# The first norm of a hybrid layer: all low parts on VectorE, the first two results' steps in between

## The chip, the cores and the metric

The kernel runs on one core of one Trainium2 chip. The core has five engines that each work through their own queue in program order and wait for each other by semaphores: TensorE (PE in the profile; PEld are its weight loads), VectorE (DVE), ScalarE (ACT), GpSimd (POOL) and SyncE (SP, which here only issues transfers). The metric is the device time of one execution in microseconds.

## The reference

One layer on 512 tokens of width 1024, batch 1, float32:

```
h = rmsnorm(x, norm1)
proj = h @ w_in            # q, k, v of A; beta, alpha; gates; f, i, q of B; g_a, g_b
o_a = gated_delta_rule(...)     # 8 heads of 128, chunkwise with a triangular solve
o_b = hgrn2_recurrence(...)     # 8 heads of 128, state with per-channel decay
x = x + (sigmoid(g_a) * (o_a @ w_a) + sigmoid(g_b) * (o_b @ w_b)) @ w_out
h2 = rmsnorm(x, norm2)
x = x + peer(h2)           # product-key top-16 experts of 16384, 8 heads
return rmsnorm(x, final_norm)
```

rmsnorm is x * rsqrt(mean(x * x) + 1e-6) * g. Only its first use, ahead of `w_in`, matters here, and the two recurrences that read the projections.

## The kernel before, in words

Rows are kept transposed: `xT` is eight chunks (c = 0 to 7) of 128 channels by 512 tokens. A float32 product is made of three matmuls on rounded parts: `hhi` and `whi` are the rounded values, `hlo` and `wlo` what the rounding left, and `piece` (line 505) issues whi by hhi, wlo by hhi and whi by hlo for one chunk. The eight pieces of one unit (128 output columns) sum in one PSUM tile. `w_raw` loads the weights of a unit, `w_cut` (line 501) splits them: ScalarE rounds (`whi`), then VectorE or GpSimd subtracts (`wlo`). Units 0 and 1 were split on VectorE, those behind them on GpSimd.

The first five units (NF = 5: a_k, a_q and three merge-gate units) start before the norm's factor is known. `unscaled` splits x times norm1, the pieces run on that, and the results are multiplied by the factor `rs` afterwards (`rescaled`, line 980). Meanwhile `squares` sums x squared into `acc` (ScalarE squares, VectorE adds), `token_scales` turns the sum into four columns `r4`, and `spread_scales` spreads them over all partitions with diagonals `rd` and matmuls; ScalarE copies the broadcast to `rs`. Then each chunk is scaled properly (`scaled`, VectorE) and split anew (`resplit`, line 456: ScalarE rounds into `hhi`, then the low part, odd chunks on GpSimd, even ones on VectorE). Unit 5 and all behind it read these. The loop at line 1050 issues this: its step k issues one piece, and at set values of k also the steps named above. The steps of the first two results (a_k and a_q: the rescaling, three convolution steps, a tanh and a product, `consume`, line 935) were issued at once at k = 12, ahead of the first `scaled`.

What follows is the mixer. Its order is decided while the program is built: `Flow` (line 136) keeps a clock for each engine from fixed costs, and the loop at line 1108 always issues the next step of that chain whose inputs its clock has ready first. The chains are `setup` (small gates, from the weights wabh and wabl), `branch_a1` and `branch_a2` (branch A; a1 prepares a head, with the transposes of a_k, kn, a_q and a_v in the tile mA; a2 doubles the inverse in iv and then carries the state SA through four blocks), `branch_b` (branch B; seven `level` steps of VectorE and ScalarE with a group of small matmuls in pl each, then the state SB) and `projections` (units 5 to 77, piece by piece). The pieces are what covers the waits of the branches; when they are used up, the branches run bare. A projection is also held back while the head's earlier results are still in use (`allowed`). Behind the mixer come the branch matrices, the second norm, the product-key search and the experts, all in fixed order.

The start times that this order sets on the chip are not Flow's: an engine waits wherever an input is not there.

Of the kernel before, what the change touches and what calls it, by code (L numbers as in the profile page):

```python
# [10 lines left out]
F32 = mybir.dt.float32  # L11
# [7 lines left out]
OP = mybir.AluOpType  # L19
# [6 lines left out]
DC = D // P  # L26
# [45 lines left out]
HEND = 3  # L72
HSTEP = 4
NDMA = 4
LISTS = (10, 26)
HSTART = 18
GPS = 4
# [201 lines left out]
def build(ctx, tc, I, O):  # L279
# [6 lines left out]
    def act(o, i, f, **kw):  # L286
        nc.scalar.activation(o, i, f, **kw)  # L287

    vec, gps, pe = nc.vector, nc.gpsimd, nc.tensor
# [15 lines left out]
    n1, n2, nf = vecs[:, 0:8], vecs[:, 8:16], vecs[:, 16:24]  # L305
# [113 lines left out]
    hhi = hpool.tile([P, DC, T], F32R, name="hhi")  # L419
    hlo = hpool.tile([P, DC, T], F32R, name="hlo")  # L420
# [19 lines left out]
    def token_scales(sums):  # L440
        for tt in range(NC_):
            mm(sums[:, 2 * tt:2 * tt + 2], acc[:, tt * P:(tt + 1) * P], ones2)
        vec.tensor_scalar(r4, sums[:, 0:8:2], 1.0 / D, EPS, OP.mult, OP.add)
        gps.tensor_tensor(r4, r4, mhalf[:, 0:NC_], OP.pow)

    def spread_scales(r, pool):
        rd = pool.tile([P, NC_, P], F32, tag="tmpP", name="rd", bufs=3)
        for tt in range(NC_):
            vec.tensor_scalar(rd[:, tt, :], ident, r4[:, tt:tt + 1], None, OP.mult)
            mm(r[:, tt * P:(tt + 1) * P], onesm, rd[:, tt, :])  # L450

    def scaled(src, g, c, r, t):
        vec.scalar_tensor_tensor(t, src[:, c, :], g[:, c:c + 1], r, OP.mult, OP.mult)
        return t

    def resplit(c, t):
        act(hhi[:, c, :], t, AF.Copy)
        (gps if c % 2 else vec).tensor_tensor(hlo[:, c, :], t, hhi[:, c, :].bitcast(F32), OP.subtract)  # L458

    hm = (hhi, hlo)  # L460
    ps = st2.enter_context(tc.tile_pool(name="ps", bufs=1, space=PSUM))
# [9 lines left out]
    N0 = len(order)  # L471
# [5 lines left out]
    raws, wts = {}, {}  # L477
# [6 lines left out]
    def w_split(raw, eng=gps):  # L484
        hi = wpool.tile([P, DC, UW], F32R, tag="whi", name="whi")
        lo = wpool.tile([P, DC, UW], F32R, tag="wlo", name="wlo")
        act(hi, raw, AF.Copy)
        if eng is None:

            act(lo, hi.bitcast(F32), AF.Copy, scale=-1.0)  # L490
            gps.dma_start(out=lo, in_=raw, accum_op=OP.add)
        else:
            eng.tensor_tensor(lo, raw, hi.bitcast(F32), OP.subtract)  # L493
        return hi, lo

    def w_raw(n):
        if n < len(order):
            kind, j = order[n]
            raws[n] = w_load(I["eut"][j] if kind == "u" else I["wu"][UNITS[kind, j]])

    def w_cut(n):
        if n < len(order):
            wts[n] = w_split(raws.pop(n), vec if n < 2 else gps if n < N0 + NDMA else None)

    def piece(p, w, c, m):
        whi, wlo = w
        mm(p, whi[:, c, :], m[0][:, c, :], c == 0, False)
        mm(p, wlo[:, c, :], m[0][:, c, :], False, False)
        mm(p, whi[:, c, :], m[1][:, c, :], False, c == DC - 1)
# [5 lines left out]
    with ExitStack() as ph:  # L515
        sb = ph.enter_context(tc.tile_pool(name="sb", bufs=1))

        def sbt(tag, bufs=1, shape=(P, T), dt=F32):
            return sb.tile(list(shape), dt, tag=tag, name=tag, bufs=bufs)

        xT = ogA
# [458 lines left out]
        def rescaled(kind, h, p):  # L980
            t = sbt("tmpA", 2)
            vec.tensor_tensor(t, p, rs, OP.mult)
            yield from consume(kind, h, t)
# [5 lines left out]
        def allowed(kind, h):  # L989
            return kind not in HEAD or free[kind] >= h + 1 - RB[kind]  # L990

        def projections():
            def some():
                while late:
                    if next(late[0], True) is None:
                        return
                    late.pop(0)

            for n, (kind, h) in list(enumerate(order[:NPROJ]))[NF:]:
                while not allowed(kind, h):  # L1000
# [6 lines left out]
                for c in range(DC):  # L1007
                    piece(p, wts[n], c, hm)
                    some()
                    if n < NF + NTWO:  # L1010
                        some()
# [6 lines left out]
                        some()  # L1018


        NF = 5
        for t in pbuf:
            gps.memset(t, 0.0)
        gps.memset(keep, 1.0)
# [5 lines left out]
        def squares(c):  # L1030
            sumsq(xT, c, sb, "tmpP", 3, vec if c in ACCV else gps)
# [3 lines left out]
        for c in range(DC):  # L1035
# [6 lines left out]
            if c == W1:  # L1042
                w_cut(1)
        w_cut(2)
        w_raw(3)
        sums = pst("mA", 1)
        r = pst("mC", 1)
        rs = sbt("tmpB", 3)
        t = None
        for k in range((NF - 1) * DC):  # L1050
            n, c = 1 + k // DC, k % DC
            if n > NF - 3:

                c, n = divmod(k - (NF - 3) * DC, 2)
                n += NF - 2
            piece(first[n], wts[n], c, hm)
            if k < DC:
                squares(k)
            if k == 1:
                w_cut(3)  # L1060
                w_raw(4)
            if k >= LB:
                next(lbs, None)
            if k == SC1:
                token_scales(sums)
                w_cut(4)
                w_raw(5)
            if k == SC2:
                spread_scales(r, sb)
                act(rs, r, AF.Copy)  # L1070

                late = [rescaled(*order[n], first[n]) for n in range(NF)]
                pair = late.pop(0), late.pop(0)
                late.insert(0, late.pop())
                next(pair[0])
                next(pair[0])
                for _ in range(8):
                    for g in pair:
                        next(g, None)
            if n == NF - 1:  # L1080
                t2 = scaled(xT, n1, c, rs, sbt("tmpP", 3))
                if c:
                    resplit(c - 1, t)
                t = t2
            if n == NF - 1 and c == 0:
                w_cut(5)
                w_raw(6)
        resplit(DC - 1, t)
        w_cut(6)
        w_raw(7)  # L1090
        for n in range(NF):
# [141 lines left out]
    def cut(o, n, i=0):  # L1233
        return stage[:, o + i * n:o + (i + 1) * n]
# [13 lines left out]
    with ExitStack() as ph:  # L1248
        rt = ph.enter_context(tc.tile_pool(name="rt", bufs=1))

        def rtile(tag, shape, dt=F32, bufs=1):
            return rt.tile([P] + list(shape), dt, tag=tag, name=tag, bufs=bufs)
# [64 lines left out]
        with ExitStack() as p2:  # L1317
# [31 lines left out]
            for u in range(3):  # L1349
                for c in range(DC):  # L1350
# [9 lines left out]
                    if u == 1 and c == 1:  # L1360
                        spread_scales(r, sb)
                        rs = rtile("rs", (T,))
# [6 lines left out]
            t = None  # L1369
            for c in range(DC):  # L1370
                t2 = scaled(x2T, n2, c, rs, cut(6144, T, c % 4))
                if c:
                    resplit(c - 1, t)
                t = t2
                if c == C4:
                    w_raw(N0 + 5)
                    w_cut(N0 + 4)
                if c == 5:
                    scores_mm(1)
# [228 lines left out]
        for s in range(NS):  # L1608
            if s in LISTS:
                chosen[LISTS.index(s) + 1] = lists(LISTS.index(s) + 1)  # L1610
            if s + 1 < NS:
# [27 lines left out]
    with ExitStack() as ph:  # L1639
# [144 lines left out]
        for i in range(-LEAD, P):  # L1784
            n = i + LEAD
# [78 lines left out]
```

## Time and profile before

| what | value |
| --- | --- |
| three runs | 2098.38, 2101.32, 2103.18 us; median 2101.32 |
| profiled execution | 2100.59 us, its span 2098.8 us |
| TensorE busy | 2020.8 us, 96% |
| VectorE, ScalarE, GpSimd busy | 1511.7, 941.7, 853.8 us |
| chain that ended last, by engine | PE 58%, DVE 14%, DMA 2% |

The span runs from the first to the last recorded instruction. In a timeline a row gives start, duration, engine, line, operation, output and inputs; what stands in brackets is the idle time ahead of it and what ended it. TensorE runs its matmuls in the order of its queue, so a wait of one holds up all behind it.

### The profile page before, as it was taken

The numbers are of one execution on the slowest core, as the hardware profiler recorded it, in microseconds if no ns is written. First come the engines' busy times: TensorE is split into PE (matmuls) and PEld (weight loads), VectorE is DVE, ScalarE is ACT, GpSimd is POOL, SyncE is SP. The second block draws the span as 40 slices with busy tenths as digits, with TensorE's granted clock in tenths as the row PEclk, the third lists the DMA queues.
The fourth block names the chain that finished last, engine by engine and source line by source line (L and its number), as shares of the span: only waits on it lengthen the run. The fifth ranks groups of instructions, "written<-read, shape, count | busy, mean of one in ns | idle before, by whom it ended". The sixth has DMA issues, their size and how long they took to land.

```text
span 2098.8 us, 34918 instructions
## 1 busy us (share of the span) xinstructions
PE 2020.8 (96%) x13182; PEld 1735.6 (83%) x13182; DVE 1511.7 (72%) x2956; ACT 941.7 (45%) x1739; POOL 853.8 (41%) x862
## 2 busy tenths in 40 slices
PE   7899999999999999999787999999999999999898
PEld 5678787887878788888776899999999989898786
DVE  7666546656662366999995578787877878788777
ACT  4555555545554323666674333333333333333234
POOL 3566646655645644211101144433334333433422
PEclk9999999999999999999998999999999999999999
DMA  3322232131223543678799799989889898998886
GB/s 133 115 73 82 63 106 73 62 98 62 84 82 97 195 156 132 175 203 193 201 336 340 263 326 338 330 325 329 323 321 323 323 336 316 327 332 302 298 294 241
DMA packets 194873, 456.84 MB, mean 218 GB/s; under 512 B 28128, under 2 KB 91776, under 8 KB 193040
## 3 DMA queue, kind: packets, MB, share of 16 engines
q1 hardware_dynamic: 96016, 231.29, 30.6%
q0 software_dynamic: 47520, 173.04, 26.3%
q10 hardware_dynamic: 51168, 50.28, 7.2%
q8 instruction: 103, 1.69, 0.3%
q14 instruction: 66, 0.54, 0.1%
HBM read 393.11 MB, written 39.40 MB: 206 GB/s over the span
## 4 chain that ended last, share of the span: by engine, by line
PE 58%; DVE 14%; DMA 2%; issue 2%; ACT 2%; POOL 0%; SPq 0%; DVEq 0%; POOLq 0%; ACTq 0%
PE y L284 23%; PE h L284 19%; PE mm L284 12%; DVE Bg L1563 2%; DMA stage<-gD 2%; DVE stage L1265 1%; DVE scr L1261 1%; DVE stage L1259 1%; DVE A L1559 1%; PE iv L284 1%; DVE oh L1313 1%; PE pl L284 1%; DVE tv L1257 1%; DVE tv L1263 1%; PE mC L284 1%
## 5 line engine op out<-in xcount | busy, mean ns | idle before, releaser
L493 POOL TENSOR_TENSOR wlo<-wraw,whi 128x1024 fp32r<-128x1024 f32 x106 | 254.9, 2405 | 270.0 <-ACT whi L287 269.7
L284 PE MATMUL h<-hhi,wlo 128*128 128x368 f32 x1024 | 339.8, 332 | 6.1 <-DMA wlo<-wraw 6.1
L284 PE MATMUL h<-hhi,whi 128*128 128x368 f32 x1024 | 341.2, 333 | 2.9 <-ACT hext L287 2.9
L284 PE MATMUL h<-hlo,whi 128*128 128x368 f32 x1024 | 340.4, 332 | 1.6 <-POOL hlo L458 1.2
L284 PE MATMUL mm<-hhi,whi 128*128 128x512 f32 x792 | 329.5, 416 | 1.0 <-ACT a_k L287 0.6
L284 PE MATMUL mm<-hlo,whi 128*128 128x512 f32 x792 | 311.8, 394 | 3.6 <-POOL hlo L458 3.0
L284 PE MATMUL mm<-hhi,wlo 128*128 128x512 f32 x792 | 310.1, 391 | 0.5 <-DMA wlo<-wraw 0.5
L284 PE MATMUL y<-vh,wh 128*128 128x512 f32 x756 | 297.0, 393 | 13.4 <-DVE wh L1732 9.4
L287 ACT ACTIVATE whi<-wraw 128x1024 fp32r<-128x1024 f32 (+1 forms) x251 | 263.3, 1049 | 101.1 <-PE mm L284 46.1
L284 PE MATMUL y<-vl,wh 128*128 128x512 f32 x756 | 299.2, 396 | 4.8 <-DVE vl L1741 4.6
L284 PE MATMUL y<-vh,wl 128*128 128x512 f32 x756 | 297.9, 394 | 0.0
L1659 POOL DMA_INDIRECT row<-eu,eidx x144 | 171.4, 1191 | 297.7 <-DVE stage L1669 284.1
L1659 POOL DMA_INDIRECT row<-ev,eidx x144 | 173.5, 1205 | 284.9 <-DVE h2g L1677 228.7
L493 DVE TENSOR_TENSOR wlo<-wraw,whi 128x1024 fp32r<-128x1024 f32 x99 | 121.3, 1226 | 170.6 <-ACT whi L287 170.6
L284 PEld LDWEIGHTS h<-hhi,wlo 128*128 128x128 f32 x1024 | 194.1, 190 | 11.6 <-DMA wlo<-wraw 7.2
L284 PEld LDWEIGHTS h<-hhi,whi 128*128 128x128 f32 x1024 | 193.7, 189 | 8.1 <-ACT hext L287 3.8
L284 PEld LDWEIGHTS h<-hlo,whi 128*128 128x128 f32 x1024 | 193.8, 189 | 2.5 <-POOL hlo L458 1.8
L287 ACT ACTIVATE hext<-h 128x368 f32<-128x368 f32 x88 | 41.9, 476 | 331.9 <-PE h L284 328.0
L284 PEld LDWEIGHTS mm<-hlo,whi 128*128 128x128 f32 x792 | 148.9, 188 | 39.6 <-POOL hlo L458 4.7
L284 PEld LDWEIGHTS y<-vh,wh 128*128 128x128 f32 x756 | 143.2, 189 | 41.0 <-issue 9.7
L284 PEld LDWEIGHTS y<-vl,wh 128*128 128x128 f32 x756 | 143.2, 189 | 37.6 <-DVE vl L1741 10.3
L284 PEld LDWEIGHTS mm<-hhi,whi 128*128 128x128 f32 x792 | 149.4, 189 | 27.7 <-ACT a_k L287 1.0
(442 smaller groups left out, 3770.4 us busy)
## 6 DMA issues: line engine op xcount, KB each, us to landing
wraw<-eut SPq DMA_DIRECT2D x128, 512.0 KB, 5.8
stage<-ev SPq DMA_DIRECT2D x126, 512.0 KB, 5.0
wraw<-wu SPq DMA_DIRECT2D x119, 512.0 KB, 4.0
stage<-gD ACTq DMA_DIRECT2D x31, 768.0 KB, 9.0
gD<-stage ACTq DMA_DIRECT2D x11, 2048.0 KB, 9.0
wlo<-wraw POOLq DMA_DIRECT2D x42, 512.0 KB, 5.5
sg<-sgD SPq DMA_DIRECT2D x16, 256.0 KB, 2.7
sgD<-tmpP SPq DMA_DIRECT2D x14, 256.0 KB, 2.1
```

Source lines behind the costliest of these rows:

```text
L284: nc.tensor.matmul(o, l, r, start=start, stop=stop)
L287: nc.scalar.activation(o, i, f, **kw)
L493: eng.tensor_tensor(lo, raw, hi.bitcast(F32), OP.subtract)
L1257: vec.max(val[:, 0:8], src)
L1259: vec.max_index(idx[:, 0:8], val[:, 0:8], src)
L1261: vec.match_replace(scr, val[:, 0:8], src, -3.0e38)
L1263: vec.max(val[:, 8:16], scr)
L1265: vec.max_index(idx[:, 8:16], val[:, 8:16], scr)
L1313: eng.tensor_tensor(oh[:, :, 0:n, :], oh[:, :, 0:n, :], oh[:, :, n:2 * n, :], OP.add)
L1559: vec.tensor_tensor(A, it[:, 0, t0:t0 + TB].rearrange("p (n u) -> p n u", u=2)[:, :, None, :].to_broadcast([P, TP, P, 2]), iov[:, None, :, ...
L1563: vec.tensor_tensor(Bg[:, q].rearrange("p n a b u -> p (n a) b u"), hi[:, p1:p1 + TP].rearrange("p n a u -> p (n a) u")[:, :, None, :].to_ ...
L1659: gps.indirect_dma_start(out=r, out_offset=None, in_=I["eu" if k < NK else "ev"], in_offset=bass.IndirectOffsetOnAxis(ap=at, axis=0))
```

## The change

All weight splits up to unit 6 go to VectorE (`NF + 2` in `w_cut`), and so do all eight low parts of rows. The split of unit 3 is issued at k = 6 in place of k = 1. Behind k = 12 only the first two steps of the first result are issued at once; the others follow one at a time per result behind each chunk's `scaled` and `resplit`. The scaled rows use the ring z (two buffers) in place of tmpP (three).

```diff
@@ -453,9 +454,9 @@
-    def resplit(c, t):
+    def resplit(c, t, engs=(vec, gps)):
         act(hhi[:, c, :], t, AF.Copy)
-        (gps if c % 2 else vec).tensor_tensor(hlo[:, c, :], t, hhi[:, c, :].bitcast(F32), OP.subtract)
+        engs[c % 2].tensor_tensor(hlo[:, c, :], t, hhi[:, c, :].bitcast(F32), OP.subtract)
@@ -500,7 +501,7 @@
-            wts[n] = w_split(raws.pop(n), vec if n < 2 else gps if n < N0 + NDMA else None)
+            wts[n] = w_split(raws.pop(n), vec if n < NF + 2 else gps if n < N0 + NDMA else None)
@@ -1056,7 +1056,7 @@
             if k < DC:
                 squares(k)
-            if k == 1:
+            if k == 6:
                 w_cut(3)
                 w_raw(4)
@@ -1074,18 +1074,17 @@
                 late.insert(0, late.pop())
                 next(pair[0])
                 next(pair[0])
-                for _ in range(8):
-                    for g in pair:
-                        next(g, None)
             if n == NF - 1:
-                t2 = scaled(xT, n1, c, rs, sbt("tmpP", 3))
+                t2 = scaled(xT, n1, c, rs, sbt("z", 2))
                 if c:
-                    resplit(c - 1, t)
+                    resplit(c - 1, t, (vec, vec))
                 t = t2
+                for g in pair:
+                    next(g, None)
             if n == NF - 1 and c == 0:
                 w_cut(5)
                 w_raw(6)
-        resplit(DC - 1, t)
+        resplit(DC - 1, t, (vec, vec))
```

(NF is also moved to the top of the file, so every line behind it stands one lower in the new kernel.)

VectorE in the opening, from the rescaling of the first result (tmpA from iv) on, before:

```order
L982 TENSOR_TENSOR tmpA_338<-iv_167,tmpB_230 128x512
L945 SCALAR_TENSOR_TENSOR tmpP_341<-a_k_340,convw_61,tmpP_341 128x511
L945 SCALAR_TENSOR_TENSOR tmpP_341<-a_k_340,convw_61,tmpP_341 128x510
L982 TENSOR_TENSOR tmpA_346<-poB_168,tmpB_230 128x512
L945 SCALAR_TENSOR_TENSOR tmpP_341<-a_k_340,convw_61,tmpP_341 128x509
L945 SCALAR_TENSOR_TENSOR tmpP_349<-a_q_348,convw_61,tmpP_349 128x511
L949 SCALAR_TENSOR_TENSOR a_k_340<-tmpP_353,tmpP_341 128x512
```

and in the changed kernel (z is a scaled chunk, tmpB is rs, wlo the split of unit 5):

```order
L983 TENSOR_TENSOR tmpA_338<-iv_167,tmpB_230 128x512
L946 SCALAR_TENSOR_TENSOR tmpP_341<-a_k_340,convw_61,tmpP_341 128x511
L454 SCALAR_TENSOR_TENSOR z_360<-ogA_110,vecs_59,tmpB_230 128x512
L946 SCALAR_TENSOR_TENSOR tmpP_341<-a_k_340,convw_61,tmpP_341 128x510
L983 TENSOR_TENSOR tmpA_363<-poB_168,tmpB_230 128x512
L494 TENSOR_TENSOR wlo_370<-wraw_308,whi_369 128x1024
L454 SCALAR_TENSOR_TENSOR z_381<-ogA_110,vecs_59,tmpB_230 128x512
L459 TENSOR_TENSOR hlo_119<-z_360,hhi_118 128x512
L946 SCALAR_TENSOR_TENSOR tmpP_341<-a_k_340,convw_61,tmpP_341 128x509
L946 SCALAR_TENSOR_TENSOR tmpP_366<-a_q_365,convw_61,tmpP_366 128x511
```

The first `scaled` stands third and not behind all steps of both results, and the split of unit 5's weights stands ahead of the second one.

TensorE in the mixer, where the last head of branch B begins its levels (pl from b_q, b_f), before. Between this pl and the fifth level's there stand 42 matmuls of projections:

```order
L565 MATMUL poB_6739<-ident_65,tmpB_6737 128x128 x4
L284 MATMUL iv_6713<-P32_144,XT_6599 32x32 x8
L284 MATMUL iv_6713<-XT_6599,P32_144 32x32 x8
L284 MATMUL pl_6815<-b_q_6491,b_f_6657 32x32 x16
L284 MATMUL mm_6767<-hhi_118,whi_6558 128x512
L284 MATMUL mm_6767<-hhi_118,wlo_6559 128x512
L284 MATMUL mm_6767<-hlo_119,whi_6558 128x512
```

and in the changed kernel (pl from z are the levels; vb, SA, vn the state chain of branch A's head 6):

```order
L285 MATMUL pl_6642<-b_q_6367,b_f_6489 32x32 x16
L285 MATMUL mC_6532<-vn_6645,kd_5482 128x128
L285 MATMUL iv_6531<-vn_6645,AT_5404 128x128
L285 MATMUL pl_6678<-z_6665 32x16 x16
L285 MATMUL pl_6721<-z_6672 32x16 x16
L285 MATMUL mC_6532<-vb_5483,XT_5879 128x128
L285 MATMUL mC_6532<-SA_6681,nw_6445 128x128
L285 MATMUL iv_6531<-SA_6681,qd_5579 128x128
L285 MATMUL pl_6752<-z_6715 32x16 x16
L285 MATMUL iv_6531<-vn_6755,AT_5404 128x128
L285 MATMUL pl_6781<-z_6746 32x16 x16
L285 MATMUL pl_6824<-z_6775 32x16 x16
```

No matmul of a projection stands between the first level and the fifth any more; all of branch A's last blocks of that head stand there.

TensorE at the end of the mixer, in the state chain of branch A's last head, before (behind the last row shown follow five pieces, then the transposes mC from ident, tmpA):

```order
L284 MATMUL mC_7583<-vb_6887,XT_7371 128x128
L284 MATMUL mC_7583<-SA_7638,nw_7572 128x128
L284 MATMUL iv_7582<-SA_7638,qd_7017 128x128
L284 MATMUL mm_7618<-hhi_118,whi_7446 128x512
L284 MATMUL mm_7618<-hhi_118,wlo_7447 128x512
L284 MATMUL mm_7618<-hlo_119,whi_7446 128x512
L284 MATMUL iv_7582<-vn_7645,AT_6806 128x128
```

and in the changed kernel:

```order
L285 MATMUL mC_7620<-vn_7642,kd_7136 128x128
L285 MATMUL iv_7619<-vn_7642,AT_7087 128x128
L285 MATMUL mC_7620<-vb_7137,XT_7412 128x128
L285 MATMUL mC_7620<-SA_7653,nw_7609 128x128
L285 MATMUL iv_7619<-SA_7653,qd_7206 128x128
L285 MATMUL mC_7620<-vn_7657,kd_7136 128x128
L285 MATMUL iv_7619<-vn_7657,AT_7087 128x128
L285 MATMUL mC_7620<-vb_7137,XT_7412 128x128
L285 MATMUL mC_7620<-SA_7662,nw_7609 128x128
L285 MATMUL iv_7619<-SA_7662,qd_7206 128x128
L285 MATMUL iv_7619<-vn_7666,AT_7087 128x128
L566 MATMUL mC_7687<-ident_65,tmpA_7685 128x128 x4
```

The nine pieces that stood between these steps now stand ahead of them.

## Rows read from the trace of the kernel before

**Rows 1.** Busy time by stretch of 100 us: PE, PEld, DVE, ACT, POOL, then the granted clock, the DMA share and GB/s.

```profile
0.00:100.00 100.00, 82.55 (x389) 59.60 (x390) 71.08 (x153) 52.48 (x97) 40.79 (x37) 0.97 0.38 126
...
600.00:700.00 100.00, 98.15 (x880) 81.13 (x881) 38.59 (x70) 47.85 (x131) 51.51 (x66) 1.00 0.33 108
```

**Rows 2.** Waits of TensorE in the first 60 us: who, for whom, total, times, longest.

```profile
PE mA L284 <- DVE acc L435: 3.0, 1, 3.0
PE mm L284 <- POOL hlo L458: 3.0, 4, 0.8
```

**Rows 3.** Timeline of VectorE, 18 to 31 us: adds of squares, the first of nine small operations, the first diagonal alone and, from a longer window, all four merged.

```profile
18.94 2.71 DVE L435 TENSOR_TENSOR acc<-acc,sq 128x512 f32<-128x512 f32 x1
...
22.55 1.49 DVE L435 TENSOR_TENSOR acc<-acc,sq 128x512 f32<-128x512 f32 x2
...
24.94 0.69 DVE L435 TENSOR_TENSOR acc<-acc,sq 128x512 f32<-128x512 f32 x1
...
26.85 0.16 DVE L362 TENSOR_TENSOR mx<-e,e 128x8 f32<-128x8 f32 x1
...
28.07 2.38 DVE L449 TENSOR_SCALAR rd<-ident,r 128x128 f32<-128x128 f32 x1
...
28.07 2.96 DVE L449 TENSOR_SCALAR rd<-ident,r 128x128 f32<-128x128 f32 x4
```

**Rows 4.** Timeline of GpSimd, 15 to 60 us.

```profile
15.88 5.22 POOL L493 TENSOR_TENSOR wlo<-wraw,whi 128x1024 fp32r<-128x1024 f32 x2 [13.20 <-ACT whi L287]
...
56.12 1.28 POOL L458 TENSOR_TENSOR hlo<-tmpP,hhi 128x512 fp32r<-128x512 f32 x1 [1.35 <-ACT hhi L287]
57.36 2.46 POOL L493 TENSOR_TENSOR wlo<-wraw,whi 128x1024 fp32r<-128x1024 f32 x1
```

**Rows 5.** One of the costliest groups of the page: the splits of weights on VectorE (count, then busy us, mean ns of one, then idle before).

```profile
L493 DVE TENSOR_TENSOR wlo<-wraw,whi 128x1024 fp32r<-128x1024 f32 x99 | 121.3, 1226 | 170.6 <-ACT whi L287 170.6
```

**Rows 6.** Timeline of ScalarE: the high part of unit 4's weights, rs (tmpB), the high part of unit 6's weights, wabh.

```profile
26.25 1.04 ACT L287 ACTIVATE whi<-wraw 128x1024 fp32r<-128x1024 f32 x1
32.61 0.60 ACT L287 ACTIVATE tmpB<-mC 128x512 f32<-128x512 f32 x1 [5.31 <-PE mC L284]
...
55.95 1.04 ACT L287 ACTIVATE whi<-wraw 128x1024 fp32r<-128x1024 f32 x1
56.90 0.29 ACT L287 ACTIVATE wabh<-wabr 128x128 fp32r<-128x128 f32 x1
```

**Rows 7.** Timeline of VectorE, 33 to 58 us: the first rescaling and convolution step, the first low part of rows and the `scaled` behind it, wabl.

```profile
33.24 0.69 DVE L982 TENSOR_TENSOR tmpA<-iv,tmpB 128x512 f32<-128x512 f32 x1 [2.21 <-ACT tmpB L287]
35.25 0.75 DVE L945 SCALAR_TENSOR_TENSOR tmpP<-a_k,convw,tmpP 128x511 f32<-128x511 f32 x1 [1.31 <-ACT a_k L287]
...
46.40 0.68 DVE L458 TENSOR_TENSOR hlo<-tmpP,hhi 128x512 fp32r<-128x512 f32 x1
47.00 0.74 DVE L453 SCALAR_TENSOR_TENSOR tmpP<-ogA,vecs,tmpB 128x512 f32<-128x512 f32 x1
...
57.22 0.33 DVE L580 TENSOR_TENSOR wabl<-wabr,wabh 128x128 fp32r<-128x128 f32 x1 [1.30 <-ACT wabh L287]
```

**Rows 8.** Timeline of TensorE: the first matmul that reads wabl.

```profile
58.02 0.39 PE L284 MATMUL mC<-hhi,wabl 128*16 128x512 f32 x1
```

**Rows 9.** Waits of TensorE between 58 and 760 us: who, for whom, total, times, longest.

```profile
PE mA L565 <- ACT kT L287: 3.8, 4, 1.7
PE trb L627 <- DVE g L403: 1.8, 1, 1.8
...
PE mC L592 <- DVE tmpA L588: 0.7, 1, 0.7
```

**Rows 10.** Timeline of the last head of branch B: VectorE's subtractions that begin two levels, and TensorE's matmuls of one level (16, of two records each).

```profile
608.48 0.69 DVE L845 TENSOR_TENSOR z<-b 128x512 f32<-128x512 f32 x1
...
610.68 0.68 DVE L845 TENSOR_TENSOR z<-b 128x512 f32<-128x512 f32 x1
...
616.36 0.89 PE L284 MATMUL pl<-z 128*32 128x16 f32 x32
```

**Rows 11.** Timeline of TensorE in the state chain of branch A's last head.

```profile
676.48 0.38 PE L284 MATMUL mC<-vn,kd 128*128 128x128 f32 x2
676.70 0.39 PE L284 MATMUL iv<-vn,AT 128*128 128x128 f32 x2
...
677.83 0.39 PE L284 MATMUL mC<-SA,nw 128*128 128x128 f32 x2
...
681.48 0.38 PE L284 MATMUL iv<-vn,AT 128*128 128x128 f32 x2
...
685.81 0.66 PE L565 MATMUL mC<-ident,tmpA 128*128 128x128 f32 x4 [0.50 <-DVE tmpA L823]
```

**Rows 12.** The same stretch, VectorE's and ScalarE's step of one block.

```profile
676.90 0.35 DVE L813 SCALAR_TENSOR_TENSOR SA<-SA,gl,mC 128x128 f32<-128x128 f32 x1 [6.41 <-PE mC L284]
678.26 0.28 ACT L287 ACTIVATE vn<-mC 128x128 f32<-128x128 f32 x1 [2.22 <-PE mC L284]
```

**Rows 13.** Busy time by stretch of 2 us, in the opening and in the product-key search, columns as in rows 1.

```profile
50.00:52.00 2.00, 1.08 (x4) 0.62 (x5) 2.00 (x3) 0.78 (x2) 1.60 (x1) 1.00 0.00 0
...
1022.00:1024.00 2.00, 0.33 (x1) 0.14 (x1) 1.24 (x5) 0.77 (x2) 0.00 (x0) 1.00 0.05 12
...
1028.00:1030.00 2.00, 2.00 (x7) 2.00 (x8) 1.93 (x6) 1.76 (x3) 0.00 (x0) 0.50 1.07 213
```

More of the change, by code (lines that the diff above doesn't have):

```diff
@@ L74 @@
 NDMA = 4
+NF = 5
 LISTS = (10, 26)
@@ L1018, in projections @@
                         some()
-        NF = 5
         for t in pbuf:
```

## The prediction

> **What bounds the kernel now.** I read the share of each engine in 100 us stretches first, then TensorE's waits, then the timelines of VectorE, GpSimd and ScalarE around them. TensorE is busy 82.6 of the first 100 us and 98.2 between 600 and 700 [rows 1]: the mixer runs at TensorE's pace, and only the opening leaves much to gain. There the large waits are 3.0 us for `acc`, the last sum of squares, and 3.0 us for the low parts that GpSimd forms [rows 2]. Behind both stands one effect: a VectorE add of 0.69 (0.80 from start to start: two take 1.49) took 2.71 us while GpSimd formed low parts of weights [rows 3, 4]. The chain that ends the opening is acc, r4, the diagonals rd, the broadcast, rs, then VectorE's steps to the last low part of the rows, which GpSimd ends at 57.40 (56.12 + 1.28) [rows 4].
>
> **The change, part by part.** VectorE takes five weight splits and four row splits from GpSimd; a weight split costs it 1.23 us against GpSimd's 2.46 [rows 4, 5].
>
> 1, the sum of squares. The split of weights 2 now runs on VectorE from 15.8 to 17.1, as their high part is there as before. Six adds at 0.80 end at 21.7, the split of weights 3 adds 1.15 (1.23 less the usual overlap), the seventh add ends at 23.5, against 25.63 (24.94 + 0.69) [rows 3]: -2.1 us.
>
> 2, the scales. From the end of acc to rs before: 33.21 - 25.63 = 7.6 us [rows 3, 6]. In it four rd took 2.96, the first alone 2.38, while GpSimd split weights 4; the last three are 0.2 each, so four take 0.8 [rows 3]. Against that VectorE now splits weights 4 itself, ahead of the nine small operations: ScalarE's high part starts 0.62 after acc and takes 1.04 [rows 6], so the small operations (1.2 us, 26.85 to 28.07) begin 2.85 after acc and not 1.22: +1.6. Sum 7.6 - 2.2 + 1.6 = 7.0, or 6.5 if the broadcast runs at full clock. rs is there at 30.1, not 33.2.
>
> 3, rescaling and splitting. Eight `scaled` at 0.67 (0.74 less the overlap), eight splits at 0.60 (46.40 to 47.00), ten steps of the two results at 0.6 to 0.75 [rows 7] and the split of weights 5 (1.15) are 18 us of VectorE. What it waits for: 1.3 us for ScalarE's two copies ahead of the first step (33.24 to 35.25 less 0.69) [rows 7], 2.3 us at the split of weights 5, whose high part ScalarE forms only behind the second result's two copies (1.3 + 1.04), and an estimated 0.9 where a split of rows stands close behind its high part. That is 22.4 us against 24.2 before (33.21 to 57.40), so the last low part ends at 52.5: -4.9 us.
>
> 4, what is late next. TensorE's second matmul on the small gate weights (before at 58.02 [rows 8]) needs `wabl`. That step now stands behind the split of weights 6, which waits for ScalarE: the last rows' high part ends 0.8 ahead of 52.5, weights 6 take 1.04 to 52.75, their split 1.23 to 54.0, wabl to 54.2, the matmul starts at 54.3: -3.7. But ScalarE forms the high part of weights 7 right behind wabh, and GpSimd may start splitting at 54.0, within 0.1 us of wabl's start. If wabl is first it takes 0.33 undisturbed, as before (57.22, with GpSimd starting at 57.36 [rows 4, 7]); if GpSimd is first, wabl waits out 2.4 us and the gain is 1.3. Either is as likely: I take -2.5, bounds -3.7 and -1.3.
>
> The Trainium skill, "SBUF — State Buffer", section "SBUF: two separate sides", calls the pair of ports that VectorE and GpSimd share an exclusive lock, held for the whole instruction by whichever starts first. The trace agrees (2.71 us for an add of 0.7). By that rule each of the nine moves is a gain and the sum would end here, at -1.3 to -3.7; it says nothing on what VectorE's longer queue and the new order delay.
>
> 5, waits inside the mixer. The planner orders everything behind the opening by its own clocks, and the order changes up to the end of the last projection unit. Between the transposes of kn and of a_q, where TensorE waited 3.8 us in all for kT [rows 9], it had 0 to 2 projection pieces as cover and now has 0 to 6, six times two or more. The gate transpose gets three pieces of cover ahead of the copy it waited 0.7 for, and `trb` (1.8) comes after less ScalarE work. Of these 6.3 us I take 4.5 as gone; bounds 0 and 6.3, since the new order can wait elsewhere.
>
> 6, the last head of branch B. The change has moved the projection pieces forward past the branches. Between its first `pl` and its fifth level TensorE had 14 pieces; now it has none. Levels follow each other on VectorE at 2.20 us (608.48 to 610.68 [rows 10]): subtract, two exponentials, two products. The order of waits on VectorE puts the first level behind the product `og`, which needs the poB transposes. From those on: 0.7, then five levels, 12 us less what overlaps. TensorE's own work there is six groups of 16 at some 0.86 (0.89 with the last one's end [rows 10]) and nine 128x128 matmuls at 0.22 (676.48 to 676.70 [rows 11]), 7.2 us. Stepping through it gives stalls of 2.0, 1.05, 1.1 and 1.3: +5.5. Bounds 0 (if the branch is already ahead) and 7.
>
> 7, the last state chain of branch A. From `mC<-vn,kd` of block 1 to the final transposes took 9.33 us (676.48 to 685.81) with nine pieces in it and a wait of 0.50 [rows 11]. Now no piece is left. The chain by itself: 0.42 to VectorE's start and 0.35, then 0.43 to ScalarE's start and 0.28, with a little for each signal 0.82 and 0.77 per half step [rows 11, 12]; twice both is 3.2, and 4.33 from the last iv (681.48) through squares, GpSimd's power and product to 685.81. That is 7.5 us with 2.5 of matmuls (eleven at 0.22), a stall of 5.0 in place of 0.5: +4.5. Bounds +4 and +5.5.
>
> 8, TensorE's clock. After a stretch busy 0.33 of 2 us the granted clock fell to 0.50, the lower level of 1.2 GHz, and stayed there for some 4 us of full work [rows 13]; at half speed that costs 1.7. Stall 7 is like that stretch; stall 6 is busy about half the time, as the opening was from 50 to 52 us at full clock [rows 13]. I take +1.7 for both, bounds 0 and 3.4.
>
> **Sum.** -2.5 - 4.5 + 5.5 + 4.5 + 1.7 = +4.7 us. The profiled execution took 2100.59 us, span 2098.8 and 1.8 around it, 0.7 under the median of 2101.32. So 2105.3 beside the one and 2106.0 beside the other; I say 2105.5.
>
> **Rivals.** A measurement of this kernel can tell about 0.2%, 4.2 us, from no change.
> The forecast, slower by 4 to 6 us: the two stalls at the mixer's end outweigh the opening. For it: both are data dependences that the order leaves bare.
> A, not slower: branches that waited now run ahead. The gain of the opening comes whole (-3.7), all 6.3 us of waits go, and head 7's levels are done early enough to cost 3: -3.7 - 6.3 + 3 + 4.5 + 0.8 = -1.7, 2099.5; with no cost at the levels 2096. It decides if VectorE reaches the levels before TensorE does the poB transposes, which the `og` product ahead of them speaks against.
> B, no change to be told: clock at full level throughout and 5.5 of the waits gone: -2.5 - 5.5 + 10 = +2, 2103. For it: the half-busy stretch that kept its clock [rows 13].
> C, slower by 9: GpSimd takes the ports ahead of wabl (-1.3) and both stalls drop the clock (3.4), with 3 of the waits gone: -1.3 - 3 + 10 + 3.4 = +9.1, 2110. Place: 54 us, 640 and 685; it decides with the 0.1 us at wabl.
> D, that the change doesn't do what it says: VectorE, with 8.9 us more work (five times 1.23, four times 0.68), ends the low parts no earlier. Then +4.7 + 2.5 = +7, 2108. Against it: without GpSimd's company the add takes 0.69 and not 2.71.
>
> **How the numbers follow.** Forecast 0.36, B 0.34, A 0.15, C 0.10, D 0.05. Faster than -4.2: only the far part of A, 0.10. Within 4.2: B, most of the rest of A, a part of the forecast's lower edge, 0.42. Slower by more: 0.48. The range leaves out the far ends of A and C: 2098 to 2111.
>
> **What would show it.** Steps 1 to 3: acc's last add ends near 23.5, rs near 30, the last hlo on VectorE near 52.5, no GpSimd work before 53. Step 4: wabl at 54.2, or 2.4 later with GpSimd's split just before it. Step 5: TensorE's waits for kT well under 3.8. Step 6: four waits of `pl` for VectorE's z in the last head, 5.5 in all. Step 7: waits of 0.3 to 0.6 at each half step and about 4 us ahead of the last mC transposes. Step 8: the 0.50 level behind these. If the waits at 6 and 7 sum to under 5 us, the forecast is wrong; if the opening gains under 1, step 4 is.

## The result, and the profile after

The changed kernel took 2122.06 us (median of four runs, 2120.20 to 2124.48), the kernel before beside it 2101.56: a ratio of 1.0102, 95% interval 1.0090 to 1.0114. The forecast was slower, 2105.5 with a range of 2098 to 2111; the direction came out, the loss is more than four times the forecast one (20.5 us against 4.7) and the time lies outside the range. The profiled execution took 2121.44 us, its span 2119.7, 20.9 longer than that of before.

The opening did what it was meant to do. VectorE's and ScalarE's timelines in the changed kernel: the seventh add of the squares, `rs`, the last low part of the rows, the split of weights 6, `wabl`.

```profile
22.98 0.68 DVE L436 TENSOR_TENSOR acc<-acc,sq 128x512 f32<-128x512 f32 x1
...
51.94 0.69 DVE L459 TENSOR_TENSOR hlo<-z,hhi 128x512 fp32r<-128x512 f32 x1 [0.15 <-ACT hhi L288]
52.88 1.23 DVE L494 TENSOR_TENSOR wlo<-wraw,whi 128x1024 fp32r<-128x1024 f32 x1 [0.25 <-ACT whi L288]
54.03 0.28 DVE L581 TENSOR_TENSOR wabl<-wabr,wabh 128x128 fp32r<-128x128 f32 x1
```

```profile
29.22 0.60 ACT L288 ACTIVATE tmpB<-mC 128x512 f32<-128x512 f32 x1 [3.89 <-PE mC L285]
```

and TensorE's first matmul that reads `wabl`, 3.65 us ahead of [rows 8]:

```profile
54.37 0.41 PE L285 MATMUL mC<-hhi,wabl 128*16 128x512 f32 x1
```

The loss lies behind it and ends with the mixer. Where a head of branch A ends, VectorE writes its result into `ogA` (line 826 before, 827 now). Heads 0, 2, 5 and 7 before:

```profile
205.74 0.74 DVE L826 SCALAR_TENSOR_TENSOR ogA<-mC,vecs,a_gate 128x512 f32<-128x512 f32 x1
...
321.13 0.72 DVE L826 SCALAR_TENSOR_TENSOR ogA<-mC,vecs,a_gate 128x512 f32<-128x512 f32 x1
...
593.24 0.74 DVE L826 SCALAR_TENSOR_TENSOR ogA<-mC,vecs,a_gate 128x512 f32<-128x512 f32 x1
...
686.50 0.75 DVE L826 SCALAR_TENSOR_TENSOR ogA<-mC,vecs,a_gate 128x512 f32<-128x512 f32 x1 [0.75 <-PE mC L565]
```

and in the changed kernel:

```profile
213.15 0.74 DVE L827 SCALAR_TENSOR_TENSOR ogA<-mC,vecs,a_gate 128x512 f32<-128x512 f32 x1
...
382.99 0.74 DVE L827 SCALAR_TENSOR_TENSOR ogA<-mC,vecs,a_gate 128x512 f32<-128x512 f32 x1
...
625.83 0.74 DVE L827 SCALAR_TENSOR_TENSOR ogA<-mC,vecs,a_gate 128x512 f32<-128x512 f32 x1
...
706.80 0.75 DVE L827 SCALAR_TENSOR_TENSOR ogA<-mC,vecs,a_gate 128x512 f32<-128x512 f32 x1 [0.89 <-PE mC L566]
```

Branch A, which started behind an opening that was 3.65 us shorter, is 7.4 us late after head 0, 62 after head 2, 33 after head 5 and 20.3 at the end. The projections ran ahead in the meantime. TensorE's timeline around the levels of branch B's last head shows what that led to:

```profile
603.75 0.40 PE L285 MATMUL mm<-hlo,whi 128*128 128x512 f32 x1
...
606.06 0.90 PE L285 MATMUL pl<-b_q,b_f 128*32 128x32 f32 x32
608.27 0.89 PE L285 MATMUL pl<-z 128*32 128x16 f32 x32 [0.67 <-DVE z L851]
610.50 1.14 PE L285 MATMUL pl<-z 128*32 128x16 f32 x32 [1.35 <-DVE z L851]
...
618.09 1.30 PE L285 MATMUL pl<-z 128*32 128x16 f32 x32 [1.16 <-DVE z L851]
621.27 1.11 PE L566 MATMUL mC<-ident,tmpA 128*128 128x128 f32 x4 [1.88 <-DVE tmpA L824]
...
624.34 0.78 PE L285 MATMUL mm<-hhi,whi 128*128 128x512 f32 x1
```

For 20 us there is no piece of a projection, and the next one stands right behind the last transposes of branch A's head 5. (The state chain between these levels is that of head 5, with heads counted from 0 as everywhere here; the listing of the new order ahead of the prediction calls it head 6.) That is no accident: the next unit in line is the gate of branch A's head 7. Its results have two buffers, and `allowed` (line 991) holds the unit until head 5 has let go of one of them. The order is fixed while the program is built, so pieces can be counted there, from the start of the mixer: in the kernel before head 5 ends after 503 pieces, and the unit, which begins at piece 520, never waits. In the changed one head 5 has not ended by piece 520, and for 14 turns of the planner the projections stand still. Windows of 4 us over that stretch and over the end of the last state chain (columns as in [rows 1]):

```profile
604.00:608.00 4.00, 2.95 (x47) 2.44 (x46) 3.35 (x7) 1.64 (x4) 3.30 (x10) 1.00 0.17 66
608.00:612.00 4.00, 2.38 (x66) 2.28 (x67) 2.96 (x9) 1.26 (x4) 3.37 (x9) 0.85 0.02 4
612.00:616.00 4.00, 2.78 (x40) 2.39 (x39) 2.33 (x8) 1.60 (x5) 2.00 (x6) 0.73 0.13 14
616.00:620.00 4.00, 2.24 (x66) 2.01 (x64) 1.41 (x4) 1.75 (x10) 1.20 (x3) 0.70 0.62 172
620.00:624.00 4.00, 2.73 (x38) 2.37 (x39) 2.91 (x7) 1.30 (x4) 0.41 (x2) 0.50 0.65 228
624.00:628.00 4.00, 4.00 (x26) 2.97 (x25) 1.69 (x5) 3.76 (x16) 1.37 (x3) 0.52 0.00 0
...
700.00:704.00 4.00, 1.65 (x11) 1.07 (x9) 0.35 (x1) 2.23 (x10) 0.49 (x3) 1.00 0.34 128
704.00:708.00 4.00, 2.03 (x8) 1.75 (x9) 1.44 (x2) 0.14 (x1) 3.42 (x3) 0.79 0.00 0
```

In the second stretch TensorE waits for the last transposes:

```profile
705.97 0.80 PE L566 MATMUL mC<-ident,tmpA 128*128 128x128 f32 x4 [3.96 <-DVE tmpA L824]
```

TensorE is busy 56 to 74% of the time between 604 and 624, and the granted clock falls to 0.50, its lower level of 1.2 GHz, and stays there through the first 4 us of full work. TensorE's waits between 58 and 760 us, which answer to [rows 9]:

```profile
PE mC L566 <- DVE tmpA L824: 5.8, 2, 4.0
PE pl L285 <- DVE z L851: 5.1, 4, 2.0
PE iv L285 <- ACT vn L288: 2.9, 3, 1.2
PE mA L285 <- ACT dec L288: 1.9, 1, 1.9
PE mA L566 <- ACT kT L288: 1.8, 2, 1.3
PE mA L285 <- DVE LT L675: 1.7, 1, 1.7
```

The waits for kT, g and the small transposes went from 6.3 to 1.8 us as forecast, and others came in their place.

To put numbers on stretches, all kernels here are read in windows of 1 us: time in which TensorE was not busy, plus busy time times what the granted clock lacks to 1. "Opening" is 0 to 58, "body" 58 to 580, "last head" 580 to 640, "end" 640 to 730 us of the span. The sum of a row overstates the difference somewhat (23.9 for before and after, where the spans differ by 20.9), since at half clock not all work takes twice as long, among other things (behind 706 us matmuls of 128x512 start 0.43 us apart at the lower level and 0.23 at the full one); it is good for telling where. Before: 16.6, 10.5, 1.7, 1.3. After: 13.5, 19.4, 13.9, 7.2. Of the after numbers the clock makes 3.1, 3.3, 5.5 and 1.7; of those before, 3.1, 0, 0 and 0.

### The profile page after: what moved, and what is told of

Its sections match the earlier page's. It is cut to its first block, busy times and chain, and to the rows that moved or that the text cites. A ratio compares the mean times of both kernels' runs of the same rounds, so it can differ in the third digit from the quotient of the medians.

```text
span 2119.7 us, 34906 instructions
## 1 busy us (share of the span) xinstructions
PE 2025.6 (96%) x13182; PEld 1738.3 (82%) x13182; DVE 1494.2 (70%) x2965; ACT 941.7 (44%) x1739; POOL 835.7 (39%) x853
## 4 chain that ended last, share of the span: by engine, by line
PE 51%; DVE 11%; DMA 2%; issue 2%; ACT 1%; POOL 0%; SPq 0%; DVEq 0%; POOLq 0%; ACTq 0%
PE y L285 23%; PE h L285 19%; PE mm L285 8%; DVE Bg L1562 2%; DMA stage<-gD 2%; DVE A L1558 1%; DVE stage L1264 1%; DVE scr L1260 1%; DVE stage L1258 1%; DVE oh L1312 1%; DMA row<-x2D 0%; DVE oh L1307 0%; DVE tv L1256 0%; DVE tv L1262 0%; DVE oh L1302 0%
## 5 line engine op out<-in xcount | busy, mean ns | idle before, releaser
L494 POOL TENSOR_TENSOR wlo<-wraw,whi 128x1024 fp32r<-128x1024 f32 x101 | 242.2, 2398 | 302.4 <-ACT whi L288 302.0
L285 PE MATMUL y<-vh,wh 128*128 128x512 f32 x756 | 296.8, 393 | 13.9 <-DVE wh L1731 9.4
L494 DVE TENSOR_TENSOR wlo<-wraw,whi 128x1024 fp32r<-128x1024 f32 x104 | 127.5, 1226 | 173.0 <-ACT whi L288 171.3
L285 PEld LDWEIGHTS mm<-hhi,wlo 128*128 128x128 f32 x792 | 151.3, 191 | 27.7 <-DMA wlo<-wraw 2.4
```

What stands on the lines that cost most here:

```text
L285: nc.tensor.matmul(o, l, r, start=start, stop=stop)
```

## The experiments

Theory "order": the opening gains its 3 to 4 us, and all the loss comes from the order that the planner chose behind it. Rivals: VectorE's longer queue delays the branches whatever the order, or each makes half. The first four kernels cross the two openings with two orders, and disturb the planner by one number.

**The changed opening with the order of before** (e1), and **the opening of before with the changed order** (e2). The planner's choice is replaced by a list of its 942 turns, recorded from the other kernel:

```diff
         while chains:
-            best = None
...
-            best[1][1] = next(best[1][0], None)
+            k, turn = int(ORDER[turn]), turn + 1
+            ch = [ch for ch in chains if ch[2] == k][0]
+            ch[1] = next(ch[0], None)
```

> The changed opening with the mixer's order of the kernel before: the 942 turns of the planner's loop are read from a list taken from the kernel before, so TensorE's order is word for word that of before from first to last; nothing of the computation is left out. Theory 'order' (the opening gains some 3 us, and all of the loss comes from the order that the planner chose behind it): 2101.6 - 3.1 = 2098.5, between 2095 and 2101, TensorE's idle time plus clock loss behind 58 us as before (some 13 us up to 686). Rival 'VectorE' (the low parts that moved to VectorE delay the branches whatever the order): 2115 or more. Rival 'half and half': about 2110.

> The other corner: the opening of the kernel before with the mixer's order of the changed kernel, from a list of its 942 turns. Theory 'order': 2122 + 3 = 2125, between 2121 and 2128. Rival 'VectorE': 2101 to 2106. Rival 'half and half': about 2113.

**One number of the planner**: in the changed kernel (e3) and in the kernel before (e4).

```diff
-BIAS = (-600, -100, -50, 0, 0)
+BIAS = (-600, -100, -50, -50, 0)
```

in e3, and -10 in place of -50 for that number in e4.

> The changed kernel with one number of the planner altered: branch B's chain gets a bias of -50 ns in place of 0, which makes the planner choose an order that is close to that of before up to its last turns. Theory 'order': between 2096 and 2102, the stalls at the last head and the last state chain gone. Rival 'VectorE': 2115 to 2122, as the opening is that of the changed kernel to the last instruction.

> The kernel before with one number of the planner altered: -10 ns for branch B's chain in place of 0. The order comes out otherwise, with six turns of the last state chain bare at the end. Theory 'order' (any small disturbance of the planner can cost as much as this change did): 2112 to 2125. Rival 'VectorE': 2101.6, unchanged within 4 us, as VectorE's work in the opening is that of before.

Measured against the kernel before (2100.99 in these runs):

| kernel | median us | ratio, 95% interval | opening | body | last head | end |
| --- | --- | --- | --- | --- | --- | --- |
| e1 new opening, old order | 2096.64 | 0.9974 (0.9965 to 0.9984) | 13.8 | 10.9 | 1.7 | 1.5 |
| e2 old opening, new order | 2122.51 | 1.0100 (1.0083 to 1.0117) | 16.8 | 16.8 | 13.0 | 8.4 |
| e3 new opening, bias -50 | 2104.64 | 1.0019 (1.0010 to 1.0029) | 13.5 | 16.7 | 1.7 | 2.0 |
| e4 old opening, bias -10 | 2119.12 | 1.0086 (1.0069 to 1.0102) | 15.6 | 15.7 | 8.5 | 8.0 |

The time goes with the order and hardly with the opening. The old order makes the new opening 4.4 us faster than before; the new order makes the old opening as slow as the changed kernel. In e4 nothing was changed but 10 ns in a table, and it costs 18 us: its projections stand still at the same unit, for five turns. e3, with the changed opening to the last instruction, has no hold-up and no bare end, though its body loses 16.7 us. It came out 2.6 us above its range: its order was expected to be close to that of before and is so only from head 5 of branch A on, while heads 0 to 4 end 16 to 53 pieces later. Against e1 this costs 6 us in the windows and 8 in the medians (e3's trace is of its fastest execution, 2100.80 us).

**What the hold-up itself is worth** (e5): the gate of head 7 three units later, so that the projections never stand still.

```diff
+    order.insert(73, order.pop(70))
     N0 = len(order)
```

> The changed kernel with one projection unit moved: the gate of branch A's last head (unit 70) is computed three units later, behind three merge-gate units, and the planner orders freely. In the changed kernel the projections stand still at unit 70, since that gate has two buffers and branch A's state chain of head 5 still holds one; for 14 turns of the planner no piece is to be had, and these are the turns of the bare levels between 604 and 622 us. Theory 'block' (the loss at the last head of branch B is this hold-up): the stretch that cost 13.9 us of idle time and clock falls to some 3, the rest as it was: 2122 - 11 = 2111. Rival 'late branch' (branch A is some 50 pieces behind the projections, and each piece that fills a stall at 610 us is missing later): the stall moves to the last state chains behind 690, which now cost 15 or more, and the time stays between 2119 and 2126.

Measured: 2125.72 us, ratio 1.0118 (1.0102 to 1.0133). The last head falls from 13.9 to 0.9, and the end rises from 7.2 to 28.8. Its waits between 580 and 740:

```profile
PE iv L285 <- DMA X<-XD: 6.3, 1, 6.3
PE mC L567 <- DVE tmpA L825: 3.9, 1, 3.9
PE iv L285 <- ACT XT L288: 2.0, 1, 2.0
```

The pieces that now fill the levels are missing when branch A's last heads run, and those are bare from the reload of the inverse (X from XD) to the final transposes. So the hold-up is where the loss shows, not what it comes from: branch A is late, and the work that can cover it is finite.

**The clock's share** (e6): the changed kernel in its own order, with matmuls added where TensorE waits.

```diff
+        def fill(p, n):
+            for _ in range(n):
+                mm(p, hhi[:, 0, 0:P], hhi[:, 0, :])
...
                 yield [z, pl]
+                if h == H - 1:
+                    fill(plt, {0: 3, 1: 6, 4: 5}.get(l, 0))
...
             yield [on, pt, ("a_gate", h)]
+            fill(pt, {5: 8, 7: 16}.get(h, 0))
```

> The changed kernel in its own order (from a list of its turns) with 38 added matmuls of 128x512 in places where TensorE waits: 3, 6 and 5 ahead of three levels of branch B's last head, 8 ahead of the last transposes of branch A's head 5, 16 ahead of those of head 7. At 0.227 us each they take about as long as the waits that they stand in, and their results are overwritten; nothing of the computation is left out. Theory 'clock' (the half-busy stretch lowers TensorE's clock, and that is some 7 of the 20 us): the granted clock stays at 1.00 from 600 to 640 and behind 706, and the time falls to 2114 to 2118. Rival 'waits only' (at the lower clock TensorE does what it would have waited for anyway): 2121 to 2124.

Measured: 2117.02 us, ratio 1.0074 (1.0058 to 1.0089), 5.0 us under the changed kernel with 8.6 us more of matmuls. Its windows of 4 us:

```profile
608.00:612.00 4.00, 4.00 (x77) 3.34 (x76) 2.96 (x9) 1.50 (x4) 3.37 (x9) 1.00 0.02 4
612.00:616.00 4.00, 1.65 (x47) 1.33 (x46) 2.34 (x8) 1.40 (x4) 1.70 (x6) 1.00 0.16 16
616.00:620.00 4.00, 4.00 (x64) 3.03 (x62) 1.11 (x3) 1.75 (x10) 1.41 (x4) 0.57 0.78 217
620.00:624.00 4.00, 4.00 (x60) 3.39 (x55) 2.92 (x7) 1.59 (x5) 0.18 (x1) 1.00 0.49 180
...
704.00:708.00 4.00, 4.00 (x20) 3.39 (x21) 0.75 (x1) 0.00 (x0) 1.52 (x1) 1.00 0.36 99
```

Where the waits are filled the clock stays up, and the end is at 1.00 throughout. Against the expectation it falls once in the last head, behind the longest wait that was left, for vn (1.9 us, in the window from 612 to 616). The clock loss of the last head and the end falls from 7.2 us (7.7 in e2, which has the same order) to 1.7. So the lower clock was a price of its own, on top of the waits. It does not fall at the same places in every execution: ahead of 580 us the changed kernel and e6 run the same instructions in the same order, and the body lost 3.3 us to the clock in the one trace and 6.5 in the other. So a clock loss read from a single trace can be off by some 3 us.

**Branch A ahead** (e7): branch A's second chain gets more weight in the planner.

```diff
-BIAS = (-600, -100, -50, 0, 0)
+BIAS = (-600, -200, -50, 0, 0)
```

> The changed kernel with one number of the planner altered: branch A's second chain (a2) gets a bias of -200 ns in place of -100. It ends head 5 after 486 pieces, not after 520, so the projections do not stand still at unit 70; up to head 3 it is as far behind as in the changed kernel. Theory 'late branch' and theory 'block' both: the stretch from 580 to 640 costs 2 to 4 us, not 13.9, the tail 1 to 3, and the time is 2099 to 2107. Rival 'the opening leaves the branches late whatever the order': 2115 or more.

Measured: 2103.24 us, ratio 1.0012 (1.0003 to 1.0021); opening 14.1, body 19.2, last head 0.8, end 2.8. With the changed opening untouched, an order that lets branch A end in time takes 18.8 of the 20.5 us back, although its body loses as much as the changed kernel's (19.4).

**The halves of the change**, each in the order of before, so that only the opening differs: all low parts on VectorE (e8), the steps of the first two results in between (e9), and of the low parts those of weights alone (e10) and those of rows alone (e11).

```diff
-            wts[n] = w_split(raws.pop(n), vec if n < 2 else gps if n < N0 + NDMA else None)
+            wts[n] = w_split(raws.pop(n), vec if n < 7 else gps if n < N0 + NDMA else None)
...
-            if k == 1:
+            if k == 6:
```

is in e8 and e10,

```diff
-        (gps if c % 2 else vec).tensor_tensor(hlo[:, c, :], t, hhi[:, c, :].bitcast(F32), OP.subtract)
+        vec.tensor_tensor(hlo[:, c, :], t, hhi[:, c, :].bitcast(F32), OP.subtract)
```

in e8 and e11, and in e9 alone, with the ring z for the scaled rows:

```diff
-                for _ in range(8):
-                    for g in pair:
-                        next(g, None)
...
                 t = t2
+                for g in pair:
+                    next(g, None)
```

> The kernel before in its own mixer order with one part of the change alone: all low parts of weights up to unit 6 and of rows go to VectorE, and the split of unit 3 is issued at k = 6; the steps of the first two results are issued at once as before, and the scaled rows stay in tmpP. Theory 'ports' (what the opening gains comes from GpSimd no longer sharing the ports with VectorE): most of the 4.4 us of the full opening with the old order, so 2096.5 to 2098.5. Rival 'steps in between' (the gain needs the steps of the first two results between the chunks): 2100 to 2103, as VectorE has 8.9 us more work ahead of the last low part.

> The other half of the change alone, in the mixer order of before: the steps of the first two results go one at a time behind each chunk's rescaling and split, and the scaled rows use the ring z; the low parts stay where they were, and so does the split of unit 3. Theory 'ports': this half gains nothing, 2099 to 2103 (steps spread out do not make VectorE's work less, and the rows' low parts start earlier by what the steps end later). Rival 'steps in between' gains on its own: 2096 to 2099.

> The kernel before in its own order with the weights' low parts up to unit 6 on VectorE (and unit 3's split at k = 6), the rows' odd low parts still on GpSimd. Theory 'ports', by the steps of the prediction: the sum of squares and the scales end some 3 us earlier and rows gain nothing: 2097 to 2099, the clock of the opening at 1.00. Rival 'rows' (the gain is in the rows' low parts): 2100 to 2102.

> The kernel before in its own order with the rows' eight low parts on VectorE and the weights' as before. Theory 'ports': a gain of 0 to 2 us, 2099 to 2101. Rival 'rows': 2096 to 2098.

The kernel before took 2100.75 us beside e5 to e8 and 2100.97 beside e9 to e12.

| kernel | median us | ratio, 95% interval | opening |
| --- | --- | --- | --- |
| e8 all low parts | 2095.10 | 0.9974 (0.9964 to 0.9985) | 11.8 |
| e9 steps in between | 2101.49 | 1.0005 (0.9996 to 1.0014) | 18.3 |
| e10 weights' low parts | 2097.02 | 0.9979 (0.9970 to 0.9988) | 12.7 |
| e11 rows' low parts | 2102.01 | 1.0005 (0.9996 to 1.0014) | 15.9 |

The gain is the weights': in e10's trace TensorE's first matmul on `wabl` starts at 54.17, 3.85 us earlier than in [rows 8]. e8 came out 1.4 us better than its range, and e11 1.0 us above the range of theory 'ports'. In e8 and e10 the clock stays at 1.00 all through the opening, in e9 the lower level takes 4.7 us. The rows' low parts add nothing alone. In e11's trace the last of them ends at 55.6, 1.8 us earlier than before, and it is given back at once: GpSimd, with the rows taken from it, is free just when VectorE comes to `wabl`. First GpSimd, then VectorE:

```profile
55.89 2.35 POOL L505 TENSOR_TENSOR wlo<-wraw,whi 128x1024 fp32r<-128x1024 f32 x1 [9.90 <-ACT whi L299]
```

```profile
56.04 2.35 DVE L592 TENSOR_TENSOR wabl<-wabr,wabh 128x128 fp32r<-128x128 f32 x1 [0.46 <-ACT wabh L299]
```

GpSimd began 0.15 us earlier, and a step of 0.28 took 2.35, so that TensorE's matmul on it came later than in [rows 8]:

```profile
58.45 0.60 PE L296 MATMUL mC<-hhi,wabl 128*16 128x512 f32 x1 [1.98 <-DVE wabl L592]
```

That is the other branch of step 4, which put its price at 2.4; here it cost 2.1 us over the undisturbed step. What the rows' low parts would gain without this meeting no run shows. The Trainium skill, "SBUF — State Buffer", section "SBUF: two separate sides", says that whoever starts first keeps the shared pair of ports for its whole instruction; these two rows agree with it.

**The good half alone, planner free** (e12): e8 without the list of turns.

> All low parts on VectorE, the steps of the first two results at once as before, and the planner free to order the mixer. Theory 'steps late' (it is the spreading of the steps that lets branch A start late in the planner's clock, and so ends at unit 70's hold-up; with the steps at once its order has no hold-up): 2093 to 2101, the stretch from 580 to 640 at 2 to 4 us. Rival 'any change of the opening throws the planner off': 2110 to 2125, with a bare stretch around 610 or behind 690.

Measured: 2094.70 us, ratio 0.9972 (0.9961 to 0.9983), faster than both kernels. The last `ogA` in its timeline of VectorE:

```profile
681.35 0.75 DVE L826 SCALAR_TENSOR_TENSOR ogA<-mC,vecs,a_gate 128x512 f32<-128x512 f32 x1 [0.75 <-PE mC L565]
```

As built, the planner's 942 turns here are those of the kernel before, one for one, so e12 is e8 over again. The steps in between, put alone into the kernel before with the planner free, give the turns of the changed kernel but for two of them; the ring z alone leaves all 942 as they were. The planner's clocks at the start of the mixer say why. In the kernel before a_q is ready at 39.4 us and the rows' last low part at 52.9; in e12 both are earlier, 36.5 and 47.6; in the changed kernel a_q comes at 44.2, 4.8 later than before, and the low part at 48.9, 4.0 earlier. The traces agree: a_q's last step ends at 47.7 us in the changed kernel and at 43.0 before, while the first piece of a projection starts 6.0 us earlier (59.70, not 65.66). From the first head on branch A is behind the pieces: head 0 ends after 156 of them, not 142.

## Why the prediction was wrong

Steps 1 to 3 held within 0.3 us: the sum of squares ended at 23.7 (said 23.5), rs at 29.8 (30.1), the last low part at 52.6 (52.5). Small misses cancel in them: from the sum to rs it took 6.2 us and not 6.6, from there on 22.8 and not 22.4. Step 4 as well: `wabl` started at 54.03, 0.05 us ahead of GpSimd, the matmul at 54.37 (said 54.3), -3.65 us. The -2.5 was a mean of two outcomes; which of them comes hangs on such a margin, and e11 happened to show the other.

In the windows the change costs 23.9 us, 19.2 more than the forecast's 4.7. Step 5 makes 13.4 of these, steps 6 to 8 together 6.4; the opening was 0.6 better.

Step 5 failed, -4.5 from waits inside the mixer. The named waits did lose 4.5 us. But the step counted only what the new order took away, though it had said that the order can wait elsewhere, and took no loss for that even at its bound of 0. In the windows the body went from 10.5 to 19.4 us, +8.9 in place of -4.5: idle time +5.6 in new waits (2.0 for z, 1.9 for dec, 1.7 for LT are the longest), clock +3.3, for which the prediction had no term.

Step 6 was right in place and wrong in cause and size. The waits for z in the last head were three, not four, and came to 3.2 us, not 5.5; around them stood waits that it did not have (1.9 for tmpA, 1.2 for vn), and the clock took 5.5: together +12.2. The cause was read off the order as pieces that had moved forward. It was a unit that could not be issued, since branch A's head 5 was late; that is a condition in the code (`allowed`), not a row of the order, and the prediction did not look for it. Whether the hold-up is lifted (e5) or filled (e6), branch A's lateness is still paid.

Step 7 held: a wait of 3.96 ahead of the last transposes, two of 0.22 at the half steps (it gave 0.3 to 0.6 for each), the end +5.9 with 1.7 of clock, against +4.5 and a share of step 8.

Step 8 was mis-sized: +1.7 for both stalls with a bound of 3.4, measured 7.2 in those two stretches and 10.5 behind the opening. The row on which it rested, 50 to 52 us half busy at full clock [rows 13], shows a stretch that kept the clock; the last head's, 20 us at 56 to 74%, did not. The step also read the other rows too simply. Ahead of the 0.50 at 1028 us stood three stretches of 2 us with 0.33, 0.25 and 0.49 us of work, not one, and the full work at the lower level lasted 3.1 us, not 4. The changed kernel's opening shows a shorter gap of the kind: TensorE waited 1.4 us for the high part of a chunk, 0.60 of 2 us were busy from 45 to 47, and the clock was at 0.50 from some 47.5 to 54. In e8 no window of 2 us from 41 to 59 had under 1.34 of work, and the clock kept 1.00. So the 3.1 us that the opening of before lost to the clock, from some 28 to 36 us, came back at another place.

Of the rivals, C pointed the right way (slower, by clock and stalls) and stopped at 2110, since its waits were those of one head. A and B were refuted. D was wrong: the last low part ended 4.8 us earlier, 52.6 for 57.4.

What stays open: why a branch that is 14 pieces late at the end of head 0 is 63 late at that of head 2. e3 and e7 start just as late, reach 53 and 56 there and win it back, so it lies in the planner's choices; no run takes that choice apart. Nor is it settled why the new opening gained 4.4 us with the old order and with the new one nothing that can be told from noise (2122.06 against e2's 2122.51); in the windows the opening is 3.3 us shorter there too, and the body 2.6 longer.

## What to carry to other kernels

Where a scheduler orders what follows, a change is two changes: freeze the order (a list of its choices will do) to measure the edit, then let it choose again. A kernel tuned by such a planner may sit on a lucky order: of the six orders in these runs that of before was the fastest, and a disturbance of 10 ns in the planner's table cost 0.9%. An edit that gains 4 us can cost 20 by the order that it sets off. Read the conditions under which a chain may not issue, and compare how far each chain has come when the covering work runs out: in e5 cover moved from one stall to another gained nothing.

## What the runs showed of the hardware

In a stretch of 20 us in which TensorE was 56 to 74% busy, with no wait above 1.9 us, the granted clock dropped to 0.50; filling its waits and those at the mixer's end with matmuls whose results nobody reads made the kernel 5.0 us faster (e6). The same instructions in the same order lost 3.3 us to the clock in one execution and 6.5 in another. And an operation of 0.28 us on VectorE that started 0.15 us behind a GpSimd operation of 2.35 took 2.35 (e11).
